# Making the low half of streamed weight blocks with ScalarE and an adding DMA instead of a VectorE subtraction

## The chip, the cores and the metric

The kernel runs on one core of one Trainium2 chip. The metric is the device time of one execution in microseconds (us). Two runs of the kernel before took 987.15 and 988.00 us, median 987.58 us.

## What is computed

One layer of a streaming encoder over 512 positions of 1024 channels, in float32. Cut to what sets the amount of work:

```python
hn = rms_norm(h, g_mix_pre)
proj = hn @ w_in                                  # 1024 -> 8192
z_sgu, z_conv, z_pool, z_gate = split(proj)
br_a = spatial_gating(gelu(z_sgu), ...) @ w_sgu_out
br_b = conformer_conv(z_conv, ...) @ w_conv_out   # GLU, depthwise conv of 31 taps, LayerNorm, silu
br_c = multiscale_pool(z_pool, ...) @ w_pool_out
merged = g0 * br_a + g1 * br_b + g2 * br_c        # gates are sigmoids of z_gate
h = h + rms_norm(merged @ w_out, g_mix_post)
hn = rms_norm(h, g_ffn_pre)
f_gate, f_up = split(hn @ w_ffn_in)               # 1024 -> 2 x 2816
h = h + rms_norm((silu(f_gate) * f_up) @ w_ffn_out, g_ffn_post)
h = h + sigmoid(h @ w_ple_gate) * (p @ w_ple)
```

All weights are read once from HBM, some 98 MB with the activations.

## The kernel before

**Layout.** Activations lie transposed: channels on the 128 partitions, the 512 positions along the free dimension. A weight block is the stationary operand of the tensor engine.

**Products.** A float32 product is made of three passes (`mm3`, line 207): high half of the weight by high half of the activation, high by low, low by high. So each weight block is needed as a high half (`hi`, rounded to float32r) and a low half (`lo`, the rest). A block of 128 x 1024 serves eight k-tiles, that is 24 matmuls of 512 columns, in the order hi, hi, lo for each k-tile: the first matmul that reads `lo` is the third.

**The weight stream.** The class `Weights` (line 172) holds a list of blocks in the order of use. For each, `_next` (line 181) loads the block on SyncE's DMA queue into `raw`, has ScalarE write `hi` by a cast, and VectorE write `lo = raw - hi` (`split`, line 162). `raw`, `hi` and `lo` are tags of the pool `stream` with three buffers each, so three blocks can be alive: the one in use and two ahead (`AHEAD = 2`). A few blocks go into other buffers instead (`w_hi`, `w_lo`), where a longer run ahead is wanted: `weights.ahead((5, 7, 9, 10)[n])` in the output projection makes up to ten blocks before the feed-forward begins. `raw` has three buffers in every case.

**Stages in time.** Pre-norm and the first GLU tiles (0 to 46 us), other GLU tiles and spatial gating (to 190), gate and branch projections with the depthwise convolution running tap by tap on VectorE behind the matmuls (to 426), LayerNorm of the convolution and its branch (to 515), output projection and its norm (to 560), feed-forward in (to 803) and out (to 924), per-layer embedding (to the end).

**What sets the order.** Up to the output projection a scheduler places the instructions; from there on the engines run inside `with order()`, in the order in which the code is written. Either way each engine takes its own instructions strictly one after the other, and an instruction that waits holds all behind it on its engine. GpSimd (POOL) runs sums of squares, the pool windows (`win`), `conv_sum` and the third branch's accumulation into `merged`.

**Places that the prediction speaks of.** In the output projection (`mix_tile`, called from line 718 on) the tiles 4 to 7 are made half of the positions at a time; ScalarE evacuates each half tile from PSUM (`o_all`) and squares it (`o_sq`), and the channel mean of those squares (`ps_stat`, one matmul) stands in TensorE's queue behind the first tile of the second half. At the start of the feed-forward, six blocks (`N_PAIR`) are multiplied k-tile by k-tile; the ninth block's halves are made in ScalarE's queue between two `swiglu` calls. In the embedding, `weights.ahead(2)` is called at `PLE_SPLIT` for the third and fourth gate block, and once more ahead of the last four.

Of the kernel before, what the change touches and what calls it, by code (L numbers as in the profile page):

```python
# [38 lines left out]

# The first GLU pairs are multiplied before the norm of x is known.  # L40
N_RAW = 3
N_FIRST = 2 * N_RAW * P
# Matrix products on nothing that raise the tensor engine's clock while the first loads run.
N_WARM = 8
# Taps of the depthwise convolution for each tile of GLU, v, gate a, pooling, gate c; and of u.
TAPS = (4, 3, 5, 3, 5)
TAPS_U = 4
# Where a norm or a piece of a residual goes between the products, counted in k-tiles.
STAT_K, STAT_A, STAT_H, STAT_F = 4, 2, 7, 2
# [5 lines left out]
class InOrder:  # L55
    """Engines whose instructions, while `on`, are issued behind all those written before them."""

# [24 lines left out]
def hybrid_block(  # L82
# [3 lines left out]
):  # L86
    """Activations live transposed (channels on partitions, the 512 positions free), so that every
    weight is a stationary operand as it lies in memory and is loaded once. A float32 product is
    three float32r passes: each operand is split exactly into a high and a low half of 12 bits."""
    nc = tc.nc  # L90
# [25 lines left out]

# [1 line left out]
    vec = const.tile([P, N_VEC + WIDTH * KT], F32, name="vec")  # L118
# [41 lines left out]

# [1 line left out]
    def split(hi, lo, src):  # L162
# [3 lines left out]
    def split_scaled(hi, lo, src, scale):  # L166
        """The halves of src * scale, scale one number per partition."""
        act_e.activation(out=hi, in_=src, func=AF.Copy, scale=scale)
        dve.scalar_tensor_tensor(out=lo, in0=src, scalar=scale, in1=hi,
                                       op0=ALU.mult, op1=ALU.subtract)  # L170

    class Weights:
# [8 lines left out]
        def _next(self):  # L181
            src, tag = self.todo.pop(0)
            n = src.shape[1]
            raw = stream.tile([P, D], F32, tag="raw", name="raw")
            nc.sync.dma_start(out=raw[:, :n], in_=src)
            if tag is None:
                hi = stream.tile([P, D], F32R, tag="hi", name="hi")
                lo = stream.tile([P, D], F32R, tag="lo", name="lo")
            else:
                hi = slot(tag, "w_hi", shape=(D,))  # L190
                lo = slot(tag, "w_lo", shape=(D,))
            split(hi[:, :n], lo[:, :n], raw[:, :n])
            self.ready.append((hi, lo))
# [21 lines left out]
    def product(ps, w, acts, hs=FULL, k0=0, last=True):  # L215
        """ps[n, t] (+)= sum over the block's k of w[k, n] act[k, t]."""
        hi, lo = w
        for i, a in enumerate(acts):
            mm3(ps[:, hs], blk(hi, i), blk(lo, i), a[:, 0, hs], a[:, 1, hs],
                k0 + i == 0, last and i == len(acts) - 1)  # L220
# [7 lines left out]

# [1 line left out]
    background = []  # L230
# [6 lines left out]
    def rsqrt(y, a, t):  # L237
        """y = 1 / sqrt(a): a bit-pattern guess, a Newton step scaled by S, a third-order step."""
        dve.tensor_scalar(out=y.bitcast(I32), in0=a.bitcast(I32), scalar1=-0.5,
                          scalar2=RSQRT_SEED, op0=ALU.mult, op1=ALU.add)  # L240
        dve.tensor_tensor(out=t, in0=y, in1=y, op=ALU.mult)
        dve.scalar_tensor_tensor(out=t, in0=t, scalar=-RSQRT_C2 * RSQRT_S, in1=a,
                                 op0=ALU.mult, op1=ALU.mult)
        dve.scalar_tensor_tensor(out=y, in0=t, scalar=RSQRT_C1 * RSQRT_S, in1=y,
                                 op0=ALU.add, op1=ALU.mult)
        dve.tensor_tensor(out=t, in0=y, in1=y, op=ALU.mult)
        dve.tensor_tensor(out=t, in0=t, in1=a, op=ALU.mult)
        dve.scalar_tensor_tensor(out=t, in0=t, scalar=-10.0 / 3.0 * RSQRT_S ** 2, in1=t,
                                 op0=ALU.add, op1=ALU.mult)
        dve.scalar_tensor_tensor(out=y, in0=t, scalar=5.0 * RSQRT_S ** 4, in1=y,  # L250
                                 op0=ALU.add, op1=ALU.mult)

    def channel_mean(sums):
        """The mean over the channels of what `sums` holds by partition, on every partition."""
        ps = psum.tile([P, T], F32, tag="pst", name="ps_stat", bufs=1)
        ps = ps[:, :sums.shape[1]]
        pe.matmul(ps, lhsT=mean_mat, rhs=sums, start=True, stop=True)
        return ps

    def inv_rms(sums, y):  # L260
        """y = 1 / sqrt(mean over the channels + eps), on every partition; eps is in the sums."""
        rsqrt(y, channel_mean(sums), t2("rs_t", sums.shape[1]))
# [6 lines left out]
    def add_square(sums, src, i, engine):  # L269
        """The i-th of the squares that are summed; the second brings eps along."""  # L270
        if i == 0:
            act_e.activation(out=sums, in_=src, func=AF.Square)
        else:
            add_sq(sums, square(src), i, engine)
# [7 lines left out]

# [1 line left out]
    C_U, C_V, C_A, C_G, C_P, C_M = 0, 8, 16, 24, 32, 40  # L284
# [56 lines left out]

# [1 line left out]
    xg = [slot("br", f"xg{k}") for k in range(KT)]  # L343
    x_sums = row("x_sums")
    first = []
# [13 lines left out]

# [1 line left out]
    h_conv = [slot("cv", f"h_conv{i}", F32) for i in range(4)]  # L361
# [67 lines left out]

# [1 line left out]
    def natural(dst, evacuate, taps):  # L431
        """dst[t, block, c] from z with the positions on partitions; yields behind each block."""
        for c in range(2):
            banks = [bank("ps_nat") for _ in range(NB)]
            for kk in range(4):
                hi, lo = weights.get()
                for b in range(NB):
                    ts = slice(b * P, (b + 1) * P)
                    for j in range(2):
                        k = 2 * kk + j  # L440
                        a = hn[k]
                        ws = slice(j * T, (j + 1) * T)
                        pe.matmul(banks[b], lhsT=a[:, 0, ts], rhs=hi[:, ws],
                                         start=k == 0, stop=False)
                        pe.matmul(banks[b], lhsT=a[:, 1, ts], rhs=hi[:, ws],
                                         start=False, stop=False)
                        pe.matmul(banks[b], lhsT=a[:, 0, ts], rhs=lo[:, ws],
                                         start=False, stop=k == KT - 1)
                drain(taps)
                if kk == 3:  # L450
                    for b in range(NB):
                        evacuate(dst, b, c, banks[b])
                yield c, kk
# [73 lines left out]

# [1 line left out]
    merged = wide_tile("merged")  # L529
# [25 lines left out]

# [1 line left out]
    z_all = wide_tile("z_all")  # L557
# [57 lines left out]

# [1 line left out]
    drain(len(background))  # L617
# [31 lines left out]

    # ---- output projection, post-norm, residual; the last tiles a half of the positions at a time,  # L650
    # so that the norm of one half runs behind the product of the other ----
    o_all = wide_tile("o_all")
# [4 lines left out]
    class Residual:  # L657
        """h += o * y tile by tile, and the halves of h * scale; the low half runs a tile behind."""

# [49 lines left out]
    with order():  # L709
# [23 lines left out]

# [1 line left out]
        banks = [bank("ps_f") for _ in range(2 * N_PAIR)]  # L735
# [92 lines left out]
    with order():  # L828
# [26 lines left out]

# [1 line left out]
        w_ple_1 = weights.get(0)  # L857
# [31 lines left out]
def _blocks(w):  # L889
    """[K, N] -> [N / 128, 128, K]: one block for each 128 outputs, its k-tiles side by side."""  # L890
    k, n = w.shape
    return w.reshape(k // P, P, n // P, P).transpose(2, 1, 0, 3).reshape(n // P, P, k)


def _wide_blocks(w):
    """[1024, 1024] -> [8, 128, 1024]: for each half of the outputs, pairs of k-tiles."""
    return w.reshape(4, 2, P, 2, T).transpose(3, 0, 2, 1, 4).reshape(8, P, D)
# [54 lines left out]
```

## Time and profile before

| What | Value |
|---|---|
| two runs | 987.15 and 988.00 us, median 987.58 |
| span of the profiled execution, first to last instruction | 984.9 us |
| TensorE matmul busy | 974.1 us |
| VectorE busy | 675.5 us |
| ScalarE busy | 347.1 us |
| GpSimd busy | 87.4 us |
| 16 DMA engines, share of the span | 30.2% for the load and store queue |
| granted TensorE clock | 1.000 |

No separate time is listed for the profiled execution; its span stands 2.7 us below the median of the runs, which is taken as what lies around a span. The profile's page gives busy time by engine, a chain of waits followed back from the last instruction, groups of instructions (an operation with its tiles and shapes, count, busy time, mean), and DMA issues with the time from issue to landing. All instructions of the helper `InOrder` carry line 69, so groups are told apart by the names of tiles. Matmul records overlap, since matmuls are pipelined: a record of 0.39 us starts every 0.227 us.

### The profile page before, as it was taken

To read this page: it belongs to the slowest core of one execution; us is meant where nothing else is said; L and a number is where in the kernel's file an instruction comes from. 1 tells how busy PE (TensorE), PEld (TensorE's weight loads), DVE (VectorE), ACT (ScalarE), POOL (GpSimd) and SP (SyncE) were. 2 spreads that over 40 slices of the span, in tenths; PEclk is the share of its full clock that TensorE was granted. 3 is DMA by queue.
4 is the path that set the end of the run, shared out by engine and by line. 5 is a ranking of instruction groups with operands and counts; after the bars stand their busy time and mean duration, and the time that the engine had idled before them with its cause. 6 is when DMAs were issued, how large, how long until landed. Compare 5 with 4: busy or idle time off the path is not lost.

```text
span 984.9 us, 11718 instructions
## 1 busy us (share of the span) xinstructions
PE 974.1 (99%) x4682; PEld 818.4 (83%) x4682; DVE 675.5 (69%) x903; ACT 347.1 (35%) x483; POOL 87.4 (9%) x64
## 2 busy tenths in 40 slices
PE   9999999899999999999999999999999999999998
PEld 6788888688888788888888998888888888888897
DVE  7998789998988799967556687554445442223675
ACT  6422333332223332246426443332232322223442
POOL 4000004000003702160000010000000000000000
PEclk9999999999999999999999999999999999999999
DMA  6433331322222232231328102323222333334312
GB/s 226 143 107 107 109 106 65 106 69 103 86 97 86 76 128 86 102 113 65 116 99 277 65 25 74 116 86 107 88 105 87 104 84 107 93 92 141 107 43 86
DMA packets 30006, 100.53 MB, mean 102 GB/s; under 512 B 3456, under 2 KB 3968, under 8 KB 29952
## 3 DMA queue, kind: packets, MB, share of 16 engines
q1 hardware_dynamic: 29808, 99.75, 30.2%
q8 instruction: 36, 0.59, 0.2%
q14 instruction: 18, 0.15, 0.0%
q10 hardware_dynamic: 144, 0.04, 0.0%
HBM read 97.68 MB, written 2.10 MB: 101 GB/s over the span
## 4 chain that ended last, share of the span: by engine, by line
PE 89%; DVE 7%; issue 2%; DMA 1%; ACT 1%; SPq 0%; DVEq 0%; ACTq 0%
PE ps_f L69 24%; PE ps_gate L69 13%; PE ps_br L69 13%; PE ps_fo L69 12%; PE ps_ag L69 5%; PE ps_pg L69 5%; PE ps_o L69 5%; PE ps_nat L69 4%; PE ps_z L69 4%; DVE lo L69 2%; DVE acc L69 1%; PE ps_pool L69 1%; PE ps_ple L69 1%; DVE v_all L69 1%; DMA first_all<-in_w_first 1%
## 5 line engine op out<-in xcount | busy, mean ns | idle before, releaser
L69 ACT CAST hi<-raw 128x1024 fp32r<-128x1024 f32 (+3 forms) x158 | 162.5, 1030 | 455.6 <-PE ps_br L69 88.4
L69 DVE TENSOR_TENSOR lo<-raw,hi 128x1024 fp32r<-128x1024 f32 (+3 forms) x158 | 201.4, 1276 | 107.5 <-ACT hi L69 106.8
L69 DVE SCALAR_TENSOR_TENSOR acc<-h_conv,vec,acc 128x511 f32<-128x511 f32 (+14 forms) x240 | 184.2, 768 | 5.1
L69 PE MATMUL ps_f<-hg,hi 128*128 128x512 f32 (+1 forms) x624 | 184.3, 378 | 0.0
L69 PEld LDWEIGHTS ps_f<-hg,hi 128*128 128x128 f32 x624 | 115.1, 188 | 21.7
L69 PE MATMUL ps_gate<-hn,hi 128*128 128x512 f32 x384 | 119.4, 392 | 0.0
L69 PE MATMUL ps_f<-hg,lo 128*128 128x512 f32 (+1 forms) x312 | 117.8, 378 | 0.0
L69 PE MATMUL ps_fo<-f,hi 128*128 128x512 f32 (+1 forms) x396 | 110.9, 366 | 0.0
L69 PEld LDWEIGHTS ps_gate<-hn,hi 128*128 128x128 f32 x384 | 72.0, 188 | 15.9 <-issue 1.0
L69 PEld LDWEIGHTS ps_fo<-f,hi 128*128 128x128 f32 x396 | 71.7, 189 | 12.2
L69 PE MATMUL ps_nat<-hi,hn 128*128 128x512 f32 x256 | 79.0, 389 | 0.0
L69 PE MATMUL ps_gate<-hn,lo 128*128 128x512 f32 x192 | 74.8, 389 | 0.0
L69 PE MATMUL ps_fo<-f,lo 128*128 128x512 f32 (+1 forms) x198 | 72.3, 365 | 0.0
L69 PEld LDWEIGHTS ps_f<-hg,lo 128*128 128x128 f32 x312 | 58.7, 188 | 11.0
L69 PEld LDWEIGHTS ps_nat<-hi,hn 128*128 128x128 f32 x256 | 48.1, 188 | 10.0
L69 DVE TENSOR_TENSOR f<-ps_f,h_inv 128x512 f32<-128x512 f32 x22 | 15.2, 689 | 56.5 <-PE ps_f L69 56.5
L69 PE MATMUL ps_nat<-lo,hn 128*128 128x512 f32 x128 | 49.8, 389 | 0.0
L69 PE MATMUL ps_ag<-hn,hi 128*128 128x512 f32 x160 | 49.5, 390 | 0.2 <-DVE sig L69 0.2
L69 PEld LDWEIGHTS ps_gate<-hn,lo 128*128 128x128 f32 x192 | 36.1, 188 | 7.6
L69 PEld LDWEIGHTS ps_fo<-f,lo 128*128 128x128 f32 x198 | 37.3, 189 | 6.0
L69 DVE TENSOR_TENSOR silu<-ps_f,h_inv 128x512 f32<-128x512 f32 x22 | 15.2, 690 | 36.0 <-PE ps_f L69 35.9
L69 PE MATMUL ps_br<-pool,hi 128*128 128x512 f32 x128 | 39.6, 389 | 0.0
(214 smaller groups left out, 1566.1 us busy)
## 6 DMA issues: line engine op xcount, KB each, us to landing
raw<-in_w_mix SPq DMA_DIRECT2D x90, 512.0 KB, 3.2
raw<-in_w_ffn_in SPq DMA_DIRECT2D x44, 512.0 KB, 3.2
raw<-in_w_ffn_out SPq DMA_DIRECT2D x16, 448.0 KB, 3.2
raw<-in_w_ffn_out SPq DMA_DIRECT2D x8, 512.0 KB, 3.5
raw<-in_w_ple_gate SPq DMA_DIRECT2D x8, 512.0 KB, 4.1
x_all<-in_xT SPq DMA_DIRECT2D x8, 256.0 KB, 6.6
h_all<-in_xT SPq DMA_DIRECT2D x4, 512.0 KB, 5.4
out_dram<-pg SPq DMA_DIRECT2D x7, 256.0 KB, 2.0
```

The lines of the kernel that those rows point to most:

```text
L69: inst = op(*args, **kw)
```

## The change

In `Weights._next` alone, the VectorE subtraction is gone. ScalarE writes `hi` as before, then makes a second pass over `raw` that writes `-raw`, rounded to float32r in the same way, into `lo`; then a DMA issued by GpSimd adds `raw` to `lo` in SBUF (source and destination both in SBUF, with `accum_op=add`). The value left in `lo` is `raw - hi`, as before. The class holds 174 blocks; splits of activations (`split`, `split_scaled`) stay as they were.

```diff
             else:
                 hi = slot(tag, "w_hi", shape=(D,))
                 lo = slot(tag, "w_lo", shape=(D,))
-            split(hi[:, :n], lo[:, :n], raw[:, :n])
+            act_e.copy(hi[:, :n], raw[:, :n])
+            act_e.activation(out=lo[:, :n], in_=raw[:, :n], func=AF.Copy, scale=-1.0)
+            nc.gpsimd.dma_start(out=lo[:, :n], in_=raw[:, :n], accum_op=ALU.add)
             self.ready.append((hi, lo))
```

The rest of the diff takes out comments and docstrings.

The built order shows the following at three places. In ScalarE's queue at the end of the output projection's whole tiles (o_all and o_sq are the evacuation and the square of a tile, 128x512 a whole and 128x256 half of the positions), before:

```order
L69 ACTIVATE o_all<-ps_o,vec 128x512
L69 ACTIVATE o_sq<-ps_o 128x512
L69 CAST hi<-raw 128x1024 x2
L69 ACTIVATE o_all<-ps_o,vec 128x256
L69 ACTIVATE o_sq<-ps_o 128x256
```

And now:

```order
L69 ACTIVATE o_all<-ps_o,vec 128x512
L69 ACTIVATE o_sq<-ps_o 128x512
L69 CAST hi<-raw 128x1024
L69 ACTIVATE lo<-raw 128x1024
L69 CAST hi<-raw 128x1024
L69 ACTIVATE lo<-raw 128x1024
L69 ACTIVATE o_all<-ps_o,vec 128x256
L69 ACTIVATE o_sq<-ps_o 128x256
```

The last two blocks of the run ahead stand, now with two passes each, ahead of the evacuation of all half tiles. In ScalarE's queue at the start of the feed-forward (silu and f belong to `swiglu`), before:

```order
L69 ACT_TABLE_LOAD
L69 ACTIVATE silu<-silu 128x512
L69 CAST f_4732<-f 128x512
L69 CAST w_hi<-raw 128x1024
L69 ACTIVATE silu<-silu 128x512
L69 CAST f_4772<-f 128x512
```

And now:

```order
L69 ACT_TABLE_LOAD
L69 ACTIVATE silu<-silu 128x512
L69 CAST f_4835<-f 128x512
L69 CAST w_hi<-raw 128x1024
L69 ACTIVATE w_lo<-raw 128x1024
L69 ACTIVATE silu<-silu 128x512
L69 CAST f_4876<-f 128x512
```

The ninth block keeps its place behind the first `swiglu`, and its second pass stands right behind the first. In GpSimd's queue at the third branch (merged), before:

```order
L614 TENSOR_TENSOR merged<-merged,br 128x512 x2
L383 TENSOR_TENSOR conv_sum<-conv_sum,acc_226 128x512
L614 TENSOR_TENSOR merged<-merged,br 128x512 x3
L383 TENSOR_TENSOR conv_sum<-conv_sum,acc_226 128x512
L614 TENSOR_TENSOR merged<-merged,br 128x512 x3
```

And now:

```order
L616 TENSOR_TENSOR merged<-merged,br 128x512
L194 DMA lo<-raw 128x1024
L385 TENSOR_TENSOR conv_sum<-conv_sum,acc_228 128x512
L194 DMA lo<-raw 128x1024
L616 TENSOR_TENSOR merged<-merged,br 128x512
L194 DMA lo<-raw 128x1024 x2
L616 TENSOR_TENSOR merged<-merged,br 128x512
```

The adding DMAs of the stream stand between sums that wait for VectorE.

## Prediction

> **What bounds the kernel now.** First the page's busy times and its chain of waits: who is never idle, and through whom does the end come?
>
> ```profile
> span 984.9 us, 11718 instructions
> PE 974.1 (99%) x4682; PEld 818.4 (83%) x4682; DVE 675.5 (69%) x903; ACT 347.1 (35%) x483; POOL 87.4 (9%) x64
> PE 89%; DVE 7%; issue 2%; DMA 1%; ACT 1%; SPq 0%; DVEq 0%; ACTq 0%
> ```
>
> TensorE (PE) is idle for 984.9 - 974.1 = 10.8 us of the whole span. That is the most that any relief of another engine can give. Then the busy times by stretch, for where those 10.8 us lie:
>
> ```profile
> 0.00:25.00 25.00, 22.91 (x84) 16.35 (x85) 19.17 (x21) 16.83 (x27) 9.95 (x13) 1.00 0.65 228
> 150.00:175.00 25.00, 23.48 (x103) 18.74 (x101) 24.89 (x24) 9.81 (x14) 8.82 (x3) 1.00 0.26 85
> 175.00:200.00 25.00, 23.22 (x109) 19.05 (x110) 24.61 (x35) 11.08 (x16) 0.00 (x0) 1.00 0.23 84
> 325.00:350.00 25.00, 24.03 (x106) 19.59 (x105) 20.99 (x22) 9.45 (x13) 15.87 (x13) 1.00 0.27 93
> 975.00:984.90 9.90, 5.94 (x49) 5.70 (x47) 3.08 (x6) 1.36 (x3) 0.00 (x0) 1.00 0.15 53
> ```
>
> The first and the last row (2.1 and 4.0 us) are the first loads and the last tile's way out. Only where VectorE (DVE) is full, in the second and third row, does TensorE miss 1.5 + 1.8 = 3.3 us that a lighter VectorE could give back, and 1.0 us more in the fourth. So VectorE is not the bound, and the question is whether the longer way to a low half still ends before TensorE asks for it. For that the timeline, around two products of the gate stage, and the chain there:
>
> ```profile
> 229.30 5.44 PE ps_gate L69 x24
> 234.74 5.44 PE ps_br L69 x24
> 240.18 5.44 PE ps_gate L69 x24
> 245.62 5.44 PE ps_br L69 x24
> 234.55 1.06 ACT L69 CAST hi<-raw 128x1024 fp32r<-128x1024 f32 x1 [4.39 <-PE ps_gate L69]
> 241.07 1.23 DVE L69 TENSOR_TENSOR lo<-raw,hi 128x1024 fp32r<-128x1024 f32 x1 [0.17 <-ACT hi L69]
> ```
>
> TensorE uses one block every 5.44 us. ScalarE (ACT) starts a new `hi` when TensorE has let a block go, because of the three buffers; two more blocks are then multiplied, and the low half is asked for two matmuls into the next: 2 x 5.44 + 2 x 0.227 = 11.3 us after the start of `hi`. Now it is there after some 2.4 us (1.06, a hand-over, 1.23). **The stream has 11.3 us, and 9 of them are slack.**
>
> **The new way, priced.** The rows for its pieces:
>
> ```profile
> L69 DVE TENSOR_TENSOR lo<-raw,hi 128x1024 fp32r<-128x1024 f32 x137 | 180.0, 1315 | 63.3 <-ACT hi L69 63.1
> L69 ACT CAST hi<-raw 128x1024 fp32r<-128x1024 f32 x137 | 144.0, 1053 | 399.3 <-PE ps_br L69 88.4 <-PE ps_gate L69 72.6 <-issue 59.6
> L69 ACT ACTIVATE silu<-silu 128x512 f32<-128x512 f32 x22 | 13.8, 627 | 3.3 <-DVE silu L69 3.3
> L69 ACT CAST f<-f 128x512 fp32r<-128x512 f32 x22 | 13.7, 624 | 16.9 <-DVE f L69 16.9
> raw<-in_w_mix SPq DMA_DIRECT2D x90, 512.0 KB, 3.2
> raw<-in_w_pool SPq DMA_DIRECT2D x4, 256.0 KB, 2.6
> h_all<-in_xT SPq DMA_DIRECT2D x4, 512.0 KB, 5.4
> q1 hardware_dynamic: 29808, 99.75, 30.2%
> ```
>
> Removed: 174 subtractions, over 200 us of VectorE, all of it beside a busy TensorE but for the 3.3 to 4.3 us above; I take 3. Added on ScalarE: 174 passes. An ACTIVATE costs what a CAST of the same size does (627 and 624 ns), so 1.05 us each; ScalarE goes from 347 to about 525 us busy and is no bound. Added on GpSimd's queue and the DMA engines: 174 adding DMAs, of which the trace shows none. Call D the time from the end of the second pass to the sum being in place; then a low half takes L = 1.05 + 1.05 + 0.1 + D from the start of `hi`.
>
> D from below: it moves 512 KB, and a plain load of that size lands in 3.2 us. It also reads what it adds to: the step from 256 to 512 KB is 0.6 us, so a second 512 KB streamed behind the first adds 1.2 and D is 4.4. If read, add and write follow one another like two loads, D = 6.4; like three, 9.6. Loads that find others in flight took 5.4 (h_all), and the adding DMA will always find the stream's own loads. So I take **D = 6.4, L = 8.6**, with 3.2 to 9.6 as ends. A price that only a page states: the Trainium skill (Collectives: The Full Stack, "The bandwidth ceiling: the fold count and why AG ≠ RS ≠ AR") has an adding transfer run at half the rate of a copy because of its second read, and (DMA: Bandwidth & Descriptors, "Anatomy of one DMA — SWDGE (gpsimd) path") a DMA issued there take 2.0 us plus bytes by 436 GB/s; with the bytes doubled that is an estimate of 4.4 us, and no run here shows it.
>
> With L = 8.6 the streaming stages, which give 11.3, cover it: no cost there. It costs where the run ahead is shorter. In the blocks ahead of the feed-forward (ACT, then PE):
>
> ```profile
> 517.23 1.05 ACT L69 CAST hi<-raw 128x1024 fp32r<-128x1024 f32 x1
> 522.69 1.06 ACT L69 CAST w_hi<-raw 128x1024 fp32r<-128x1024 f32 x1
> 542.82 1.05 ACT L69 CAST hi<-raw 128x1024 fp32r<-128x1024 f32 x1 [1.98 <-DMA raw<-in_w_ffn_in]
> 543.77 0.47 ACT L69 ACTIVATE o_all<-ps_o,vec 128x256 f32<-128x256 f32 x1
> 544.40 0.48 ACT L69 ACTIVATE o_all<-ps_o,vec 128x256 f32<-128x256 f32 x1
> 551.21 0.59 PE L69 MATMUL ps_stat<-o_sums,mean_mat 128*128 128x256 f32 x2
> ```
>
> Twelve blocks are made from 517.23 to 542.82 here, through three `raw` buffers. **A raw buffer is now held until the adding DMA has read it**, and the next load into it waits: a turn is 3.2 for the load plus L, 11.8 us. The third block (w_hi, 522.69) shifts to 523.9 behind the second block's own extra pass; the twelfth is three turns later, its passes starting at 523.9 + 3 x 11.8 = 559.3 and ending at 561.4. Behind them in ScalarE's queue stand the evacuations of the half tiles, 0.63 us a pair of o_all and o_sq. Four pairs and the last sum on VectorE (0.4) bring the squares to 564.4, and TensorE waits with `ps_stat`, which it reached at 551.21: **13.2 us**. It holds the products behind it; by then the feed-forward's blocks are complete, so nothing is added there.
>
> Four other places, each with the start of `hi` and the first use of the low half:
>
> ```profile
> 603.99 1.05 ACT L69 CAST w_hi<-raw 128x1024 fp32r<-128x1024 f32 x1
> 607.45 0.39 PE L69 MATMUL ps_f<-hg,w_lo 128*128 128x512 f32 x1
> 930.78 1.99 ACT L69 CAST w_hi<-raw 128x1024 fp32r<-128x1024 f32 x2
> 936.54 0.28 PE L69 MATMUL ps_pg<-h,w_lo 128*128 128x256 f32 x1
> 954.65 1.98 ACT L69 CAST hi<-raw 128x1024 fp32r<-128x1024 f32 x2
> 959.15 0.39 PE L69 MATMUL ps_pg<-h,lo 128*128 128x512 f32 x1
> 302.01 1.04 ACT L69 CAST hi<-raw 128x1024 fp32r<-128x1024 f32 x1
> 308.47 0.39 PE L69 MATMUL ps_z<-hn,lo 128*128 128x512 f32 x1
> 465.79 1.04 ACT L69 CAST hi<-raw 128x1024 fp32r<-128x1024 f32 x1
> 471.99 0.39 PE L69 MATMUL ps_br<-conv,lo 128*128 128x512 f32 x1
> ```
>
> - Ninth block of the feed-forward: 3.46 us are there, 8.6 needed: **5.1**. The next blocks' starts in the same queue leave them enough behind this shift.
> - Fourth gate block of the embedding: its passes start at 930.78 + 2.1, so it is ready at 941.5 for 936.54: **4.9**.
> - First of the last four blocks: 4.5 there, **4.1**.
> - A `w_pool` block is half as long, and ScalarE is late there behind the pool's split: 6.46 there, 2.1 missing, at each of four such blocks: **8.6** (taken alike).
> - First branch block of the convolution, behind ScalarE's swishes: 6.2 there, **2.4**.
>
> Sum: 13.2 + 5.1 + 4.9 + 4.1 + 8.6 + 2.4 = 38.3, less 3 for VectorE: 984.9 + 35.3 = 1020.2 us of span, and with the 2.7 us between span and median **1023 us**, 3.6% slower.
>
> **Rivals.** *The adding DMA is short (not slower).* With D = 4.4 (L = 6.6) the terms are 7.1 (a turn of 9.8, three of them 6.0 less), 3.1, 2.9, 2.1, 0.6 and 0.4, 16.2 less 3: 1001 us; with D = 3.2 and all of VectorE's 4.3 us, 991 to 993. It decides for "same" up to D of about 5. For it: a lone store or load here is short. Against it: it is never alone, and a software-issued add is nothing that the trace shows. The Trainium skill's 4.4 us, as estimated above, comes out here as well, at 1001 us.
>
> *The adding DMA is long.* From L = 11.3, D = 9.1, the whole stream is late: a buffer's turn is L + 5.44 over three blocks, so every us more costs a third of a us a block. At D = 9.6 the local terms grow to 22.7, 8.3, 8.1, 7.3, 21.4 and 5.6; the stream pays 0.17 at some 110 blocks, 18 us, and the feed-forward's second half, whose three blocks take 22 x 3 x 0.227 = 15.0 against a turn of 17.2, another 18: 109 less 3, 1094 us. Bandwidth does the same: the loads hold the 16 engines for 30.2% of the span, 297 us or 1.6 of each 5.44; if an add takes three times a load, 6.3 do not fit into 5.44 and 174 blocks cost 140 us, 1130. For it: an add that reads twice already brings the engines to about 90%. Against it: that is still under one.
>
> *GpSimd's queue blocks the stream.*
>
> ```profile
> POOL conv_sum L383 <- DVE acc L69: 120.9, 6, 38.8
> ```
>
> An adding DMA behind such a sum waits with it, up to 38.8 us by this row if VectorE were as late as now. But VectorE loses a fifth of its work just there, so this I price with the long case, at one such wait less the 2.7 us that L leaves of 11.3: 36 us more, 1059.
>
> *VectorE's relief decides.* At most 10.8 us if all else is hidden, 977; realistically 983.
>
> **How the numbers follow.** Covered stream with local costs (D from 5 to 9), 1023 us, own range 1007 to 1080: 0.46. Short DMA: 0.24. Long DMA or blocked queue: 0.27. Relief decides, 0.02; the add does not run beside the rest at all (built otherwise than said), 0.01, slower. A change of less than 2% is about what a measurement of this kernel cannot tell from none. Faster 0.02, since all idle time together is 1.1%; same 0.25, the short case and the lower edge of the forecast; slower 0.73. The range goes from the lower end of D, 993, to 1150, which takes in the long case up to engines just overfull.
>
> **What would show it.** Right: `lo` rows of VectorE gone, DVE near 460 us, ACT near 525; TensorE with waits of 5 to 13 us at `ps_stat` before the feed-forward, at its ninth block, at the gates and near the end, and none in the steady feed-forward. From the end of `lo` on ScalarE to TensorE's release there, D of 5 to 9. Wrong: D under 5 and TensorE's idle time under 25 us; or blocks coming every 6 us or more in the steady feed-forward, which is the long case.

## The result and the profile after

The changed kernel takes **1052.30 us** (median of 1051.70 and 1052.89) against 987.58: ratio **1.0656**, 95% interval 1.0636 to 1.0677. It is 6.6% slower. The profiled execution took 1051.7 us, its span is 1049.6.

The page after, in the order in which that of before was read: busy times, the two DMA queues (packets, MB, share of 16 engines), the DMA issues.

```profile
span 1049.6 us, 12143 instructions
...
PE 992.1 (95%) x4682; PEld 830.8 (79%) x4682; DVE 483.8 (46%) x729; ACT 504.2 (48%) x657; POOL 228.9 (22%) x238
...
q0 software_dynamic: 25056, 89.14, 47.7%
q1 hardware_dynamic: 29808, 99.75, 29.0%
...
lo<-raw POOLq DMA_DIRECT2D x137, 512.0 KB, 5.8
raw<-in_w_mix SPq DMA_DIRECT2D x90, 512.0 KB, 4.1
```

VectorE lost 192 us of work and ScalarE gained 157, and neither sets the end: TensorE does, as before. Two things happened to it. Its idle time went from 10.8 to 1049.6 - 992.1 = 57.5 us, which is 46.7 more. And its busy time for the same 4682 matmuls went from 974.1 to 992.1, which is 18.0 more. Together they are the 64.7 us of span. The queue of adding DMAs (q0) holds the 16 engines for 47.7% of the span, more than all loads together, and the loads now land in 4.1 us where they took 3.2.

What TensorE waits for (who waits, for what; us in total, times, longest):

```profile
PE ps_stat L69 <- DVE o_sums L69: 21.3, 1, 21.3
PE ps_fo L69 <- DMA lo<-raw: 7.6, 2, 5.7
PE ps_pool L69 <- ACT pl_hi L69: 4.3, 2, 3.0
PE ps_pg L69 <- DMA w_lo<-raw: 3.9, 2, 2.6
PE ps_o L69 <- DMA w_lo<-raw: 2.2, 1, 2.2
PE ps_br L69 <- DMA lo<-raw: 2.0, 2, 1.0
PE ps_stat L69 <- DVE f_sums L69: 1.8, 1, 1.8
PE ps_nat L69 <- DMA lo<-raw: 1.8, 2, 1.4
PE ps_o L69 <- DMA lo<-raw: 1.6, 2, 1.4
PE ps_br L69 <- ACT hi L69: 1.6, 1, 1.6
...
PE ps_f L69 <- ACT hi L69: 1.3, 1, 1.3
PE ps_f L69 <- DMA w_lo<-raw: 1.2, 1, 1.2
...
PE ps_pg L69 <- DMA lo<-raw: 0.7, 1, 0.7
```

Few waits, each at a place where blocks are made in a hurry. The stretches of the span show the same, and the second loss beside it (busy times by engine, then the granted clock, DMA share, GB/s):

```profile
350.00:375.00 25.00, 22.00 (x91) 17.70 (x90) 18.86 (x26) 11.21 (x13) 5.66 (x6) 0.93 0.74 181
575.00:600.00 25.00, 12.71 (x93) 12.53 (x94) 12.14 (x31) 12.50 (x27) 2.58 (x3) 0.69 0.62 152
700.00:725.00 25.00, 25.00 (x112) 20.71 (x111) 5.54 (x8) 10.80 (x14) 4.30 (x5) 1.00 0.86 192
950.00:975.00 25.00, 15.65 (x77) 14.05 (x75) 1.12 (x2) 12.39 (x16) 5.11 (x6) 0.80 0.97 230
```

In the steady feed-forward (third row) TensorE is full, at clock 1.00, with the DMA engines 0.86 busy: there the longer way to a low half costs nothing. Where TensorE has waited longest, its clock is under 1. Finer stretches around the longest wait's end, at 587.28 us:

```profile
587.00:588.00 1.00, 0.71 (x3) 0.63 (x3) 0.23 (x1) 0.41 (x2) 0.00 (x0) 0.50 0.99 279
588.00:589.00 1.00, 1.00 (x6) 0.91 (x5) 0.43 (x1) 0.00 (x0) 0.00 (x0) 0.50 1.08 217
...
591.00:592.00 1.00, 1.00 (x11) 1.00 (x10) 0.93 (x3) 0.00 (x0) 0.00 (x0) 1.00 0.00 0
```

For some 3.3 us after the wait the clock stays at 0.50, and six matmuls are done in a us where eleven are done afterwards. Taken over all stretches of half a us, busy time by (1 - granted clock) adds up to 14.9 us, against 0.0 before. It lies in eight places, each behind a wait or two. About 3 of the 18 us of longer busy time stay unexplained by this sum.

And the chain of waits through the burst of blocks ahead of the feed-forward (start us, us, what):

```profile
535.92 9.58 DMA raw<-in_w_mix
...
552.66 7.46 DMA lo<-raw
...
560.19 4.29 DMA raw<-in_w_ffn_in
...
566.80 9.46 DMA w_lo<-raw
...
576.31 5.83 DMA raw<-in_w_ffn_in
...
582.22 1.04 ACT hi L69
...
587.28 1.22 PE ps_stat L69 x2
```

This is the turn of a raw buffer that the prediction described: adding DMA, then the load that it let in, then ScalarE's passes, then the next adding DMA, three times over, and at the end the evacuations and the channel mean. But its pieces are long: adds of 7.5 to 9.5 us, loads of 4.3 to 9.6.

### The profile page after: what moved, and what is told of

Read it like the earlier page. It is cut to its first block, busy times and chain, and to the rows that moved or that the text cites. A ratio compares the mean times of both kernels' runs of the same rounds, so it can differ in the third digit from the quotient of the medians.

```text
span 1049.6 us, 12143 instructions
## 1 busy us (share of the span) xinstructions
PE 992.1 (95%) x4682; PEld 830.8 (79%) x4682; DVE 483.8 (46%) x729; ACT 504.2 (48%) x657; POOL 228.9 (22%) x238
## 3 DMA queue, kind: packets, MB, share of 16 engines
q0 software_dynamic: 25056, 89.14, 47.7%
## 4 chain that ended last, share of the span: by engine, by line
PE 70%; DMA 12%; issue 10%; ACT 3%; DVE 3%; POOL 0%; POOLq 0%; ACTq 0%; SPq 0%
PE ps_f L69 19%; PE ps_br L69 10%; PE ps_gate L69 10%; PE ps_fo L69 8%; PE ps_nat L69 6%; PE ps_ag L69 5%; DMA lo<-raw 5%; PE ps_first L69 3%; PE ps_z L69 3%; DMA w_lo<-raw 3%; DVE acc L69 2%; PE ps_pg L69 2%; DMA raw<-in_w_mix 1%; PE ps_pool L69 1%; DMA raw<-in_w_ffn_in 1%
## 5 line engine op out<-in xcount | busy, mean ns | idle before, releaser
L194 POOL DMA_DIRECT2D lo<-raw x157 | 137.2, 874 | 608.5 <-ACT lo L69 586.6
L69 DVE SCALAR_TENSOR_TENSOR acc<-h_conv,vec,acc 128x511 f32<-128x511 f32 (+14 forms) x240 | 193.7, 807 | 6.9
L69 ACT ACTIVATE lo<-raw 128x1024 fp32r<-128x1024 f32 (+1 forms) x157 | 161.9, 1031 | 3.6 <-PE ps_first L69 3.6
L69 PE MATMUL ps_fo<-f,hi 128*128 128x512 f32 (+1 forms) x396 | 115.3, 377 | 0.0
L69 PEld LDWEIGHTS ps_fo<-f,hi 128*128 128x128 f32 x396 | 75.5, 200 | 12.1
L69 PE MATMUL ps_fo<-f,lo 128*128 128x512 f32 (+1 forms) x198 | 74.8, 378 | 7.6 <-DMA lo<-raw 7.6
L69 PEld LDWEIGHTS ps_fo<-f,lo 128*128 128x128 f32 x198 | 39.8, 201 | 14.1 <-DMA lo<-raw 8.0
L69 DVE TENSOR_TENSOR f_sums<-f_sums,sq 128x512 f32<-128x512 f32 (+1 forms) x7 | 4.3, 616 | 95.9 <-ACT sq L69 95.9
```

The source lines that it names most:

```text
L69: inst = op(*args, **kw)
L194: nc.gpsimd.dma_start(out=lo[:, :n], in_=raw[:, :n], accum_op=ALU.add)
```

## The experiments

All times are set against the kernel before. The edits are in `_next`, unless said otherwise.

| Run | us | ratio (95%) | TensorE's wait at `ps_stat`, us |
|---|---|---|---|
| the change | 1052.30 | 1.0656 (1.0636 to 1.0677) | 21.3 |
| e1: VectorE adds, no DMA | 992.75 | 1.0055 (1.0035 to 1.0075) | 1.3 |
| e2: DMA copies, no add | 1015.92 | 1.0290 (1.0269 to 1.0310) | 14.1 |
| e3: subtraction in the first burst | 1020.34 | 1.0335 (1.0265 to 1.0404) | 0.3 |
| e4: subtraction in the first burst and from block 155 on | 997.07 | 1.0102 (1.0085 to 1.0119) | none |
| e5: TensorE kept busy | 1047.88 | 1.0613 (1.0598 to 1.0627) | 1.6 |
| e6: `h_all` issued later | 1052.24 | 1.0670 (1.0643 to 1.0697) | 20.9 |
| e9: no `h_all` loads | 1046.16 | 1.0595 (1.0575 to 1.0614) | 20.4 |
| e10: four raw buffers | 1033.56 | 1.0467 (1.0448 to 1.0486) | 11.1 |
| e12: control for e10 | 1046.98 | 1.0603 (1.0583 to 1.0623) | 21.3 |
| e7: change in the steady feed-forward only | 990.56 | 1.0033 (1.0020 to 1.0045) | none |
| e8: change where VectorE is full only | 985.60 | 0.9982 (0.9974 to 0.9991) | none |
| e11: e8 and four blocks more | 985.46 | 0.9980 (0.9971 to 0.9989) | none |

**e1: ScalarE's passes without the DMA.**

```diff
-            nc.gpsimd.dma_start(out=lo[:, :n], in_=raw[:, :n], accum_op=ALU.add)
+            dve.tensor_tensor(out=lo[:, :n], in0=raw[:, :n], in1=lo[:, :n], op=ALU.add)
```

> ScalarE still makes both passes, but VectorE adds raw to the negated high half instead of a DMA. If the lateness of the adding DMA is what costs (my theory): 985 to 995 us, hardly any wait at ps_stat ahead of the feed-forward. If the second ScalarE pass is what holds back the evacuations behind it (rival): over 1030 us, with the wait at ps_stat of 15 us or more still there.

Measured: 992.75 us. Its busy times:

```profile
PE 975.8 (98%) x4682; PEld 819.7 (83%) x4682; DVE 676.4 (68%) x903; ACT 503.5 (51%) x657; POOL 85.8 (9%) x64
```

And TensorE's longest wait in it:

```profile
PE ps_pool L69 <- ACT pl_hi L69: 3.3, 1, 3.3
```

ScalarE does all that it does in the change (503.5 us), and it costs 5 us in all. The rest of the loss, 60 of 65 us, comes with the DMA. One wait is ScalarE's own, though: at `ps_pool` the pool's split (`pl_hi`, 335.02 us) stands right behind an extra pass (334.06), without any adding DMA.

**e2: the same DMA without the add.**

```diff
-            nc.gpsimd.dma_start(out=lo[:, :n], in_=raw[:, :n], accum_op=ALU.add)
+            nc.gpsimd.dma_start(out=lo[:, :n], in_=raw[:, :n])
```

> The DMA from SBUF to SBUF copies raw over lo and adds nothing, so the low half of every streamed block is the whole block instead of the rest (the output is not the reference's); all else is as in the changed kernel. If the second read of the adding DMA makes it long (my theory): issue to landing falls from 5.8 to about 4.6 us, its share of the 16 engines from 48% to about 25 to 30%, and the time to 1020 to 1035 us. If what makes it long is that GpSimd issues it (rival): landing 5.5 us or more and 1045 us or more.

Measured: 1015.92 us, shorter than expected of either theory, since the copies land sooner than I took:

```profile
q0 software_dynamic: 25056, 89.14, 24.6%
...
lo<-raw POOLq DMA_DIRECT2D x137, 512.0 KB, 2.9
...
raw<-in_w_mix SPq DMA_DIRECT2D x90, 512.0 KB, 3.3
```

For the same 89.14 MB an add holds the engines 47.7% of 1049.6 us and a copy 24.6% of 1014.0: 501 against 249 us, twice as long; an add lands in 5.8 us, a copy in 2.9. The loads, too, are back near the 3.2 us of before. That an add reads its destination as well fits this factor of two. Still, a copy that only holds the raw buffer leaves a wait of 14.1 us at `ps_stat`. The Trainium skill (Collectives: The Full Stack, "The bandwidth ceiling: the fold count and why AG ≠ RS ≠ AR") puts an adding transfer at half the rate of a copy: these two rows agree. The estimate of 4.4 us for one add, worked out from the Trainium skill (DMA: Bandwidth & Descriptors, "Anatomy of one DMA — SWDGE (gpsimd) path"), stands against 5.8 measured.

**e3 and e4: the old subtraction where blocks are made in a hurry.** e3 has the condition `89 <= i <= 103`, e4 the one shown; i counts the blocks in their order.

```diff
+            i = 173 - len(self.todo)
+            if 89 <= i <= 103 or i >= 155:
+                split(hi[:, :n], lo[:, :n], raw[:, :n])
+            else:
+                act_e.copy(hi[:, :n], raw[:, :n])
...
```

> The old subtraction for 15 blocks alone, those made ahead of the feed-forward and its first three (90th to 104th of 174); the adding DMA for the other 159. If the loss sits where the run ahead is short (my theory): 1010 to 1020 us, since 28 us of idle TensorE between 525 and 650 us go, and some 9 us of slow clock with them. If it is spread over the stream because the DMA engines are 77% busy (rival): above 1040 us.

> As the one before, and the old subtraction for the last 19 blocks too (the end of the feed-forward's second half and the embedding), the adding DMA for the other 140. My theory: 990 to 996 us, what is left being the pool stage and the first branch block of the convolution. Rival (spread over the stream): above 1025 us.

Measured: e3 1020.34 us (its two times, 1014.5 and 1026.2, lie far apart, at a mean granted clock of 0.991 and 0.981; the profiled one is the shorter), e4 997.07, one us more than I expected. e4's queue of adding DMAs:

```profile
q0 software_dynamic: 20160, 71.71, 40.3%
```

And its longest waits:

```profile
PE ps_pool L69 <- ACT pl_hi L69: 4.0, 2, 3.0
PE ps_nat L69 <- DMA lo<-raw: 1.9, 2, 1.4
PE ps_br L69 <- DMA lo<-raw: 1.9, 2, 1.0
```

Taking the adding DMA from 34 of 174 blocks gives back 55 of the 65 us, and TensorE's busy time falls from 992.1 to 976.2 us with the waits. The other 140 adds still hold the engines for 40.3% of the span and cost 1%. The loss is local, as predicted; it isn't bandwidth over the whole span.

**e5: does the wait itself lower the clock?** In the output projection, ahead of the channel mean (`N_BUSY` is 90):

```diff
+                ps = psum.tile([P, T], F32, tag="pst", name="ps_busy", bufs=1)
+                for _ in range(N_BUSY):
+                    pe.matmul(ps, lhsT=warm_up[:, :P], rhs=warm_up, start=True, stop=True)
                 y = t2("o_inv", H)
                 inv_rms(o_sums[:, lo_half], y)
```

> The changed kernel with 90 matmuls of a constant tile put into TensorE's queue ahead of the channel mean (ps_stat) for which it waits 21.3 us before the feed-forward; their result is read by nobody, and 90 x 0.227 = 20.4 us fits into the wait. My theory, that the lower granted clock behind this wait (0.69 and 0.83 in the two stretches of 25 us, about 10 us of lost work) follows from TensorE's standing idle: the clock stays at or near 1.00 there, the idle time in the profile is filled, and the time falls to 1040 to 1046 us, with ps_stat starting no later. Rival, that the lower clock comes from the load of the DMA engines or of the other engines, and only falls in the same place: the clock is still under 0.9 there and the time is 1050 us or more.

Measured: 1047.88 us. The stretches around the wait:

```profile
565.00:575.00 10.00, 9.93 (x55) 5.58 (x56) 0.00 (x0) 3.70 (x5) 1.72 (x2) 1.00 1.04 204
575.00:585.00 10.00, 9.95 (x47) 4.56 (x47) 0.69 (x1) 5.94 (x8) 1.72 (x2) 1.00 0.93 220
585.00:595.00 10.00, 8.36 (x63) 7.25 (x61) 7.47 (x19) 4.84 (x15) 0.86 (x1) 1.00 0.60 156
```

In the change, the second of the three stretches was:

```profile
575.00:585.00 10.00, 0.00 (x0) 0.00 (x0) 0.81 (x2) 6.02 (x10) 2.21 (x3) 0.50 0.88 207
```

With the DMA engines as full as in the change (1.04 and 0.93 against 0.99 and 0.88) the clock stays at 1.00 as long as TensorE has something to do, where the change shows 0.74, 0.50 and 0.73 in the same three stretches. So here standing idle lowers the clock, not the load of the others. In size I was wrong: I read a mean clock of 0.69 in 25 us as 10 us lost, but that mean holds the waiting time, in which a low clock costs nothing. In stretches of half a us the loss behind this wait is 1.5 us (and 1.7 more behind the wait of 2.2 us at `ps_o` before it); the other 2.9 of the 4.4 us gained are within what e12 below shows to be scatter.

**e6 and e9: the residual's loads in the burst.** e6 wrote the four loads of `h_all` (2 MB) behind the run ahead; e9 leaves them out:

```diff
     for k in range(0, KT, 2):
-        nc.sync.dma_start(out=h_all[:, k:k + 2], in_=xT[:, k:k + 2])
+        nc.gpsimd.memset(h_all[:, k:k + 2], 0.0)
```

> The changed kernel with the four loads of h_all (2 MB) issued behind the weight loads of the run ahead instead of in front of them. My theory, that the burst of weight blocks before the feed-forward took 8 us more than I predicted because those 2 MB went through DMA engines that were already full: TensorE's wait at ps_stat falls from 21.3 to 12 to 16 us and the time to 1036 to 1045 us. Rival, that the held raw buffers alone set the length of the burst: the wait stays at 19 to 22 us and the time at 1049 to 1054.

> The changed kernel without the four loads of h_all: GpSimd fills h_all with zeros instead, so the residual input is left out of the sum and the output is another. In the run before, the four loads were issued at 525.3 to 526.8 us, hardly earlier than without that edit (526.5 to 528.9), so it did not move them and tested nothing. My theory, that the burst of blocks ahead of the feed-forward runs at what the 16 DMA engines can do (12 blocks of a load and an adding DMA, and these 2 MB on top, some 6 us of them at the 294 to 400 GB/s that this stretch shows): TensorE's wait at ps_stat falls from 21 to 13 to 17 us and the time to 1043 to 1048. Rival, that only the three raw buffers and the latency of each transfer set its length: the wait stays at 19 to 22.

Measured: e6 1052.24 us and a wait of 20.9, but its edit put the loads at the same time as before, so it decides nothing. e9: 1046.16 us, and a wait of 20.4 where I expected 13 to 17. The wait is no good measure there, for TensorE now came to it 5 us earlier. The burst's length is one: from the third block's `w_hi` (first row) to the channel mean (second row).

```profile
530.02 1.04 ACT L69 CAST w_hi<-raw 128x1024 fp32r<-128x1024 f32 x1
...
581.24 1.22 PE L69 MATMUL ps_stat<-o_sums,mean_mat 128*128 128x256 f32 x2 [20.42 <-DVE o_sums L69]
```

That is 51.2 us; with the loads it was 587.28 - 531.66 = 55.6 in the change. In e6, with the loads, it was 54.4. So the 2 MB lengthen the burst by some 3 to 4 us, not 8: my theory was half right in size and wrong about the wait.

**e10 and e12: a fourth raw buffer.** e12 has the two smaller pools alone. (`bufs=4` stands also where three raw buffers are taken for the first loads.)

```diff
-    tmp = ctx.enter_context(tc.tile_pool(name="tmp", bufs=6))
-    stat = ctx.enter_context(tc.tile_pool(name="stat", bufs=2))
+    tmp = ctx.enter_context(tc.tile_pool(name="tmp", bufs=5))
+    stat = ctx.enter_context(tc.tile_pool(name="stat", bufs=1))
...
-            raw = stream.tile([P, D], F32, tag="raw", name="raw")
+            raw = stream.tile([P, D], F32, tag="raw", name="raw", bufs=4)
```

> The changed kernel with four raw buffers instead of three; to find the room, the pool tmp has five buffers instead of six and stat one instead of two. Theory of this prediction, that the burst is long because a raw buffer is held until its adding DMA has read it: a turn of about 16 us then serves four blocks and not three, so the wait at ps_stat falls from 21 by at least 8 us, to under 13. Rival, that the DMA engines are full there (share 0.83 to 1.05 in the windows of the burst), so a fourth buffer only lengthens the line in front of them: the wait is still 17 us or more. The two smaller pools are judged by the control beside it.

> Control for the fourth raw buffer: the changed kernel with three raw buffers, and with the pool tmp at five and stat at one as there. If the smaller pools do little, the wait at ps_stat stays at 20 to 22 us and the time at 1050 to 1058 us; what they cost beyond that is taken off the other run.

Measured: 1033.56 us with four, 1046.98 with three. The same two rows with four, then with three:

```profile
530.87 1.05 ACT L69 CAST w_hi<-raw 128x1024 fp32r<-128x1024 f32 x1
...
574.88 1.22 PE L69 MATMUL ps_stat<-o_sums,mean_mat 128*128 128x256 f32 x2 [11.09 <-DVE o_sums L69]
```

```profile
529.71 1.05 ACT L69 CAST w_hi<-raw 128x1024 fp32r<-128x1024 f32 x1
...
585.39 1.22 PE L69 MATMUL ps_stat<-o_sums,mean_mat 128*128 128x256 f32 x2 [21.25 <-DVE o_sums L69]
```

44.0 us with four buffers, 55.7 with three. So that three buffers are held makes the burst long, as the prediction had it: one buffer more takes back 11.7 of the 27 us by which it outlasts that of before (551.21 - 522.69 = 28.5). Full DMA engines alone would have left it as long; they make the pieces longer, not the number of turns. The control is also a warning: its median is 5.3 us under the change, which I did not expect, though its burst is as long. Its own two runs lie 3.9 us apart (1045.02 and 1048.93), the four of e6 6.9. The traces show one source of such scatter: the same wait of 3.0 us at `ps_pool` is followed by a clock of 0.50 in the change, e5, e6, e10 and e12, and by one of 1.00 in e3, e4 and e9. So times a few us apart (e5, e9) tell nothing here, and the traces must.

**e7, e8 and e11: the change only where it should be free, or of use.** The conditions for the subtraction are `i < 104 or i > 150`, `i < 28 or i > 42` and `i < 24 or i > 42`.

> ScalarE's two passes and the adding DMA only for the 47 blocks of the steady feed-forward (from the sixteenth block of its input product to two thirds of its output product); all other blocks keep the VectorE subtraction. My theory, that an adding DMA whose 8.6 us lie inside the 11.3 us of run ahead costs nothing and the relief of VectorE gives nothing there: 986 to 989 us, the same as before, with no wait of TensorE above 1 us that the kernel before had not. Rival, that every adding DMA costs a little wherever it is: 990 us or more (the 140 that remained in the run before cost some 9 us, so 47 would cost 3).

> ScalarE's two passes and the adding DMA only for the 15 blocks (29th to 43rd) whose halves are made from about 140 to 220 us, where VectorE is full in the kernel before and TensorE loses 3.3 us to it; all other blocks keep the subtraction. My theory: TensorE's two gaps there go away and nothing is lost elsewhere, 984 to 986 us. Rival, that the adding DMA gives no relief by itself (the gaps have another cause) or costs as much there in late low halves: 987 to 990 us.

> ScalarE's two passes and the adding DMA for the 25th to 43rd block, four more than in the run that used the 29th to 43rd (985.6 us); the rest keeps the subtraction. There 1.1 and 0.65 us of TensorE's gaps were left between 150 and 200 us, because VectorE is already behind when the first of those blocks comes. If earlier relief takes the rest away: 983.5 to 985 us. Rival, that one of the four added blocks is late itself (the changed kernel had a wait of 1.4 us for a low half at 141 us): 985.5 to 987 us.

Measured: e7 990.56 us, 3.3 more than before where I expected none. Its profile places one wait at the first blocks of the stretch, where three blocks are made in a row, and nothing between 675 and 900 us:

```profile
617.26 0.50 PE L69 MATMUL ps_f<-hg,lo 128*128 128x512 f32 x1 [1.44 <-DMA lo<-raw]
```

TensorE misses 1.7 us there (with 0.2 for a `hi`). Nearly all of the rest is one wait for VectorE, long before the first of the 47 blocks is made, that the kernel before had not:

```profile
42.32 0.50 PE L69 MATMUL ps_ag<-hn,hi 128*128 128x512 f32 x1 [1.65 <-DVE hn L69]
```

So the trace gives the rival, a small cost of every add, nothing; what this one wait comes from was not tried. e8: 985.60 us, the interval just under one. VectorE's stretches, of before 1.5 and 1.8 us short, are now 1.1 and 0.65 short:

```profile
150.00:175.00 25.00, 23.91 (x105) 19.15 (x103) 24.89 (x24) 9.80 (x14) 8.95 (x4) 1.00 0.24 79
175.00:200.00 25.00, 24.35 (x115) 20.24 (x116) 24.58 (x36) 13.74 (x19) 2.19 (x3) 1.00 0.50 133
```

e11, which begins four blocks earlier, has 0.69 and 0.40 us missing there and a new wait of 0.7 us for a low half: 985.46 us, where I expected 983.5 to 985; that is no more than e8 gives. With 1.7 to 2.1 us (0.2%), both beat the kernel before and the change, by intervals that just exclude no difference.

## Why the prediction was right, and where its numbers were off

Right was the mechanism: the adding DMA lands inside the 11.3 us that the stream gives, raw buffers are held longer, and it is at the hurried places that TensorE waits. The row for `lo` (5.8 us, median of 137, most of them in the steady stream, and 0.3 us from ScalarE's end to the issue in the chain) makes D 6.1, where 6.4 was taken. DVE near 460 came out at 483.8 and ACT near 525 at 504.2. The forecast of 1023 us was 29 too low. By place, in us of TensorE's waiting:

| Step of the prediction | taken | measured |
|---|---|---|
| burst ahead of the feed-forward | 13.2 | 21.3, and 3.8 at `ps_o` |
| ninth block of the feed-forward | 5.1 | 2.5 |
| fourth gate block | 4.9 | 2.6, and 1.3 at the third |
| first of the last four blocks | 4.1 | 0.7 |
| pool stage | 8.6 | 3.3 more than before |
| first branch block of the convolution | 2.4 | 2.6, and 0.9 at the next |
| end of the feed-forward | nothing | 7.6 + 1.8 |
| spatial gating | nothing | 1.8 |
| VectorE's relief | -3 | -3.3 |
| **sum** | **35.3** | **46.9** (46.7 by busy time) |
| lower clock after waits | nothing | 18.0 of busy time, 14.9 of it by the clock's rows |

- **The burst was mis-sized.** The prediction made a turn of 3.2 for the load and 8.6 for L, 11.8 us, three times. From the third block's passes (531.66) over the sixth's (550.38) and ninth's (564.50) to the twelfth's (582.22) the turns took 18.7, 14.1 and 17.7 us, 50.6 in all. In the last turn of the chain the add takes 9.46 instead of 6.4 and the load 5.83 instead of 3.2, together 5.7 more: the load was priced as in the kernel before and the add as two such loads, while several of each share the engines here (share 0.83 to 1.05 in stretches of 10 us between 535 and 585). The three turns outlast the 35.4 taken by 15 us; `h_all` is some 3 to 4 of them. TensorE waited only 8 us longer than forecast, since it came to `ps_stat` later itself (3.8 us of waits at `ps_o` on the way, and the slow clock behind them). That the buffers are what is waited for stood up to e10, and e2 shows the size that goes with a shorter hold (from the third block's `w_hi` at 524.96 to `ps_stat` at 568.24, 43.3 us).
- **A second burst was overlooked.** At the end of the feed-forward the blocks of the embedding are made between the last blocks of `w_ffn_out`. In the trace of before, that is where ScalarE's casts stand close together. The prediction has this place in no sum: its long case prices the second half of the feed-forward as late throughout, and not these blocks. It cost 7.6 + 1.8 us of waiting, and e4 got it back.
- **The clock was left out.** The prediction counted a wait at its own length. A wait of 21 us, but also one of 3.0 us in the pool stage and one of 2.2 at `ps_o`, is followed by some 3 us at half clock. The Trainium skill (TensorE: Matmul & The Clock Gate, "What's actually happening") describes this: half rate after an idle window of about 3.4 us, until a busy one has passed. The trace agrees in the half rate (0.50), and has it after shorter waits too: 2.2 us here, and in e4 one of 1.3 us at 621 us.
- **Four local terms were too high.** In the pool stage the cause was another: not the `w_pool` blocks' low halves but `pl_hi`. In e1 its cast stands behind an extra pass of ScalarE; in the change, ahead of the wait of 3.0 us, ScalarE itself stood idle for 4.18 us until VectorE's `win` was there, which came behind the convolution's taps. What made it late isn't shown. At the ninth block the low half was there 6.8 us after the start of `hi` (641.53 to 648.36), not 8.6. Ahead of the last four blocks the low half had 7.8 us where 4.5 were counted (`hi` starts at 1015.17, TensorE asks at 1022.97). Each term was worked out as if TensorE kept its old distance to ScalarE; a plausible reading, not tested, is that the earlier waits had moved it. These four (pool stage, ninth block, fourth gate block, first of the last four) were 13.6 us too high together, and the waits that the sum has no term for come to 17.2. That the sum of the waits is only 11.6 us too low is in part luck.

The rivals: the short DMA (D near 4.4) falls by the landing of 5.8. Bandwidth over the whole span falls by the full rows of the steady stream at a DMA share of 0.86, and by e4; together the queues hold 77% of the engines, where about 90% were feared. (Its 6.3 against 5.44 us for 174 blocks would be 150 us, not 140.) GpSimd's queue did block the stream in the change, but at one place and not for long. In spatial gating the first sum of `conv_sum` waited 7.8 us for VectorE, which had itself waited 4.4 us for an adding DMA (`w_lo`); the adding DMA behind it went out at 137.36 us, though ScalarE's pass for it had ended at 131.9, and TensorE waited 1.4 us for its low half. The chain there:

```profile
136.14 0.52 POOL conv_sum L383
...
137.36 4.57 DMA lo<-raw
141.97 27.04 PE ps_nat L69 x118
```

The other waits of `conv_sum` are of 4.4 us at most, where one of before was 38.8, and of TensorE's waits for a low half at the convolution's branch blocks (0.9 and 1.0 us) the adds were issued within 0.3 us of ScalarE's passes. So this rival was real and its price was not 36 us but 1.4.

VectorE's relief was there in full, 3.3 us, and decided nothing in the change; alone, in e8 and e11, it is worth about 2.

## What to carry to other kernels

A longer way that fits into the steady run ahead is free only there: before taking it, find every place where blocks are made faster than they are used, and price it with the transfers competing and with the time that each staging buffer is held. In these traces a wait of TensorE of 3.1 us or more cost its length and then some 2 us more in half clock (14.9 us over eight places in the change); a shorter one did so in some runs and not in others. Relief of an engine that is full in one stretch is worth having in that stretch alone: the same edit on 15 of 174 blocks gains 0.2%, on all of them it loses 6.6%.

## What the runs showed of the hardware

- An adding DMA of 512 KB from SBUF to SBUF lands in 5.8 us (median of 137, beside the stream's loads) and a plain copy in 2.9; in a burst of three an add took up to 9.5. Per transfer an add holds the 16 engines for 501 us / 174 = 2.9 us and a copy 1.4. GpSimd is busy for 0.87 us with the issue of an add, 0.54 with that of a copy.
- Loads suffer from them: 4.1 us instead of 3.2 beside adds, 3.3 beside copies.
- TensorE's granted clock was 0.50 after every wait of 3.1 us and more in these traces, in the change for some 3 to 5.5 us each time. A wait of 3.0 us at `ps_pool` was followed by it in five traces and not in three, and one of 1.3 us was in e4. The clock stayed at 1.00 where TensorE was kept busy beside equally full DMA engines (e5).
